# The gated MLP's entry: the scale's scratch moved to another buffer, the late sums queued behind half_x, the last output weights' residues formed by VectorE

## The chip, the cores and the metric

The kernel runs on one core of a Trainium2 chip. The metric is the device time of one execution in microseconds. The core has five engines that each take their instructions in order: TensorE (PE, with its weight load PEld), VectorE (DVE), ScalarE (ACT), GpSimd (POOL) and SyncE (SP, which here issues the DMAs). [...]

## The reference

The kernel computes two layers of a causal decoder over 16 learned meta tokens and 1024 tokens of width 1024. Layer 0 mixes with a short gated convolution and a gated DeltaNet, layer 1 with sliding-window attention. Each layer ends in the part that this change is about, a gated MLP of width 2816 with a causal width-3 convolution on the gate:

```python
def rms_norm(x, w):
    xf = x.astype(jnp.float32)
    y = xf * lax.rsqrt(jnp.mean(xf * xf, -1, keepdims=True) + EPS)
    return (y * w.astype(jnp.float32)).astype(x.dtype)

def conv_ffn(h, w_up, conv_w, w_down):
    gate, val = jnp.split(h @ w_up, 2, -1)
    gate = causal_dwconv(gate, conv_w)
    return (jax.nn.silu(gate) * val) @ w_down
...
for layer in range(DEPTH):
    ...
    h = h + mix.astype(h.dtype)
    ff = conv_ffn(rms_norm(h, ffn_norm_w[layer]), ffn_w_up[layer], ffn_conv_w[layer], ffn_w_down[layer])
    h = h + ff.astype(h.dtype)
```

## The kernel before

Activations lie transposed: eight tiles `h[k]` of 128 channels by 1040 tokens. A float32 product is made of three reduced-precision products: each operand is rounded to a high part (ScalarE) and what is left, the low part, is formed by a subtraction (VectorE or GpSimd); high x high, high x low and low x high are summed in PSUM.

**The MLP (`ffn`).** The tokens are taken as two halves s = 0, 1 of `hf` = 520 (layer 0) or 516 (layer 1) columns. The up projection is done by a seven-product scheme of the Strassen kind: instead of eight block products of inner size 512 there are seven, j = 0 to 6, whose moving operands `X[j][0..3]` are blocks of the normalised input or sums of blocks, and whose weights are blocks of the raw weights `wg`, `wv` or their sums `sa`, `sb`. `parts(j, k, ...)` (L746) makes one operand tile: high part by ScalarE (L750, or L753 with the norm's weight), low part by VectorE (L751 or L754). X0, X1 and X6 come straight from `h`; X2 (`t2`), X3, X4 and X5 need sums by VectorE: L784 and L785 for X2 and X3, L792 for X4, L795 for X5. The 28 operand tiles take five slots of the pool `xb` and slots of `big`, which holds 24 tiles, among them the eight of `h`; slots for the last operands come free only when `h` tiles have been used up.

At the entry also stand the sums of squares for the RMS norm (squares by ScalarE at L740, added up by VectorE in L741, the two halves of a tile `r`), and `scales(s)` (L757) for each half: four matmuls with a matrix of ones into a PSUM tile `C` (L760), then a reciprocal square root by two Newton steps, alternating ScalarE (L763, L764, L766) and VectorE (L767, L768), into `rstd`. Its scratch tiles are `sg`, `th` (which the convolution uses later) and `rs_y`, which has the tag and the one buffer of the snapshot `u2`. `rstd` is first used in L896.

Then a loop over 22 blocks i of 128 hidden channels. Each takes PSUM accumulators from two rings of two, `A` and `C`, and runs its seven products, 24 matmuls each, in this program order: A = X0 (weights w1; snapshot `p1`), C' = X1 (w1; added to `p1` into `r` by L866), A += X2 (w2; snapshot `u2`, a ScalarE copy at L826), C = X3 (w2), A += X4 (w3; snapshot `u3`), then the X0 product of block i+1, A += X5 (w3), C += X6 (w4). A snapshot must be taken before the next product adds to `A`. Weights come by two DMAs per block (L833), are summed (L869, L870, L879, L887), and are split by `wsplit` (high L809, low L810) into a ring of three pairs of tiles. Block 0's and every even block's raw weights share a ring of two buffers with the weight loads of the stage before. The gate then goes through L895, L896, the convolution (L851 to L855) and a multiplication (L898), and a DMA (L899) writes the block to DRAM. The down projection follows in a second part.

**The stage before the second MLP (`swa`).** At its end `outputs(1, yb, QCH[2:])` makes the last 346 tokens of the attention's output projection: four weight loads by `load_w` (L128: DMA L131, high part by ScalarE L134, low part by GpSimd L135, 128x1024 elements), each followed by two groups of 12 matmuls (L147), whose PSUM results VectorE adds into `h` (L1205). Two PSUM buffers are in use there for these groups.

**What sets the order.** The source gives the program order, and a planner that simulates the engines' times chooses the order of instructions within each engine's queue when the program is built, and when buffers are handed on; so instructions of a later line can stand ahead of earlier ones. `with tc.issue_after(ins):` adds one constraint: the instructions of the block that run on `ins`'s own engine come after `ins` in that engine's queue. It adds no semaphore.

Of the kernel before, what the change touches and what calls it, by code (L numbers as in the profile page):

```python
# [2 lines left out]

# [4 lines left out]
F32 = mybir.dt.float32  # L8
# [4 lines left out]
ALU = mybir.AluOpType  # L13
# [5 lines left out]
KT = D // P  # L19
# [8 lines left out]
QCH = [(14, 334)] + CH[1:]  # L28
# [54 lines left out]
def trunk(tc, hT0, w_in, w_ab, w_out, w_q, w_k, w_v, w_o, w_up, w_down, vec, cst, out):  # L83
    nc = tc.nc
    pe, ve, ac, gp, sp = nc.tensor, nc.vector, nc.scalar, nc.gpsimd, nc.sync
    ctx = ExitStack()
    with ctx:
# [38 lines left out]
        def aux(name, tag="b"):  # L126
            return banks["in"].tile([P, 512], F32, tag=tag, name=name, bufs=banks[tag])

        def load_w(src, nk, name):
            raw = wp.tile([P, nk, P], F32, tag="wraw", name=name + "r")  # L130
            sp.dma_start(raw, src)  # L131
            hi = wp.tile([P, nk, P], F32R, tag="whi", name=name + "h")
            lo = wp.tile([P, nk, P], F32R, tag="wlo", name=name + "l")
            ac.copy(hi, raw)  # L134
            gp.tensor_tensor(lo, raw, hi.bitcast(F32), ALU.subtract)  # L135
            return hi, lo

        def gemm(w, xs, c0, n, ks=None, ring=None):
# [567 lines left out]
        def ffn(h, layer, last):  # L706


            hf = 516 if last else 520
# [7 lines left out]
            with tc.tile_pool(name=f"fx{layer}", bufs=5, side="right", reuse_waits="tile") as xb:  # L717
                with tc.tile_pool(name=f"f{layer}", bufs=1, reuse_waits="tile") as fp, \
                        tc.tile_pool(name=f"fu{layer}", bufs=2, space=PSUM, reuse_waits="tile") as pu:

                    def half(tag, bufs, name=None):
                        return fp.tile([P, hf], F32, tag=tag, name=name or tag, bufs=bufs)
# [5 lines left out]
                    def full(tag, bufs=1):  # L728
                        return fp.tile([P, 2 + 2 * hf], F32, tag=tag, name=tag, bufs=bufs)
# [11 lines left out]
                                ve.tensor_tensor(ss[s], ss[s], sq, ALU.add)  # L741

                    X = [[None] * 4 for _ in range(7)]

                    def parts(j, k, src, vcol=None):

                        t = (xb if 4 * j + k < 5 else big).tile([P, T], F32R, tag="big", name=f"X{j}{k}")
                        hi, lo = t[:, 0:hf], t[:, hf:2 * hf]
                        if vcol is None:
                            ac.copy(hi, src)  # L750
                            ve.tensor_tensor(lo, src, hi.bitcast(F32), ALU.subtract)  # L751
                        else:
                            ac.activation(hi, src, AF.Copy, scale=vcol)  # L753
                            ve.scalar_tensor_tensor(lo, src, vcol, hi.bitcast(F32), ALU.mult, ALU.subtract)  # L754
                        X[j][k] = (hi, lo)

                    def scales(s):  # L757
                        ps = wide("C")
                        for b in range(2):
                            pe.matmul(ps[:, b, :q], ones, ss[s][:, b * q:b * q + q], start=True, stop=True)  # L760
                        a, t = (x[:, :hf] for x in (full("sg"), full("th")))
                        y = half("u2", 1, "rs_y")
                        ac.activation(two(a), ps[:, :, :q], AF.Identity, scale=1.0 / D, bias=epsc)  # L763
                        ac.activation(y, a.bitcast(I32), AF.Exp, scale=-0.5 * LN2 / (1 << 23), bias=seed)  # L764
                        for i, (sc, m3) in enumerate(((1.0, -3.00033), (0.25, -0.75))):
                            ac.activation(t, y, AF.Square, scale=sc)  # L766
                            ve.tensor_tensor(t, a, t, ALU.mult)  # L767
                            ve.scalar_tensor_tensor(rstd[:, tk[s]] if i else y, t, m3, y, ALU.add, ALU.mult)  # L768

                    w = [col(V_FN + 8 * layer + k) for k in range(KT)]  # L770

                    B = lambda i, k, s: h[4 * i + k][:, tk[s]]
# [7 lines left out]
                    t2 = [half("t2", 2, "t2") if k < 2 else vt2[:, (k - 2) * hf:(k - 1) * hf] for k in range(4)]  # L780
# [5 lines left out]
                        parts(2, k, t2[k])  # L786
                    for k in range(4):
                        parts(3, k, B(0, k, 0))
                    for s in range(2):
                        scales(s)  # L790
                    for k in range(4):
                        ve.scalar_tensor_tensor(B(0, k, 1), B(1, k, 1), w[4 + k], B(0, k, 1), ALU.mult, ALU.subtract)  # L792
                        parts(4, k, B(0, k, 1))
                    for k in range(4):
                        ve.scalar_tensor_tensor(B(1, k, 0), B(1, k, 0), w[4 + k], t2[k], ALU.mult, ALU.subtract)  # L795
                        parts(5, k, B(1, k, 0))
                        parts(6, k, B(1, k, 1), w[4 + k])

                    nw = [0]

# [6 lines left out]
                    def wsplit(t, at, n, src):  # L807
                        hi, lo = (x[:, at:at + n, :] for x in t)
                        ac.copy(hi, src)  # L809
                        ve.tensor_tensor(lo, src, hi.bitcast(F32), ALU.subtract)  # L810
# [48 lines left out]
                    for i in range(NF):  # L859
                        (wg, wv), w1, A, p1 = nxt  # L860
                        g1, g2, v1, v2 = wg[:, 0:4], wg[:, 4:8], wv[:, 0:4], wv[:, 4:8]
                        Bk = wide("C")
                        product(Bk, w1, 4, 1, True)
                        r = full("r", 2)
                        ve.memset(r[:, 0:2], 0.0)
                        ve.tensor_tensor(two(r[:, 2:2 + hf]), Bk[:, :, :q], two(p1), ALU.add)  # L866

                        sa = fp.tile([P, KT, P], F32, tag="ws", name="sa", bufs=2)
                        ve.tensor_tensor(sa[:, 4:8], v1, v2, ALU.add)  # L869
                        ve.tensor_tensor(sa[:, 0:4], sa[:, 4:8], g1, ALU.subtract)  # L870
                        w2 = wtile()
                        wsplit(w2, 0, KT, sa)
                        product(A, w2, 0, 2, False)
                        u2 = snap("u2", A)
                        C = wide("C")
                        product(C, w2, 4, 3, True)

                        sb = fp.tile([P, KT, P], F32, tag="ws", name="sb", bufs=2)
                        ve.tensor_tensor(sb[:, 0:4], g1, v1, ALU.subtract)  # L879
                        w3 = wtile()  # L880
                        wsplit(w3, 0, 4, sb[:, 0:4])
                        wsplit(w3, 4, 4, v2)
                        product(A, w3, 0, 4, False)
                        u3 = snap("u3", A)
                        v = full("v")
                        ve.tensor_tensor(two(v[:, hf:2 * hf]), two(u3), C[:, :, :q], ALU.subtract)  # L886
                        ve.tensor_tensor(sb[:, 4:8], sa[:, 0:4], g2, ALU.subtract)  # L887
                        if i + 1 < NF:
                            nxt = first(i + 1)
                        product(A, w3, 4, 5, False)  # L890
                        ac.copy(two(v[:, :hf]), A[:, :, :q])
                        w4 = wtile()
                        wsplit(w4, 0, 4, sb[:, 4:8])
                        product(C, w4, 0, 6, False)
                        ve.tensor_tensor(two(r[:, 2 + hf:]), two(u2), C[:, :, :q], ALU.subtract)  # L895
                        ve.tensor_tensor(r[:, 2:], r[:, 2:], rstd[:, o0:], ALU.mult)  # L896
                        sg = conv(i, r)
                        ve.tensor_tensor(sg, sg, v[:, :2 * hf], ALU.mult)  # L898
                        sp.dma_start(yd[i], sg)  # L899
# [37 lines left out]
        def swa(h, sqp):  # L937
# [5 lines left out]
            with tc.tile_pool(name="l1", bufs=1, reuse_waits="tile") as lp:  # L943
# [14 lines left out]
                for i in range(4):  # L958
                    a = lp.tile([P, 192], F32R, name=f"vxh{i}")
# [227 lines left out]
                def parts(G, ys, cs):  # L1187
                    for c0, n in cs:
                        sl = slice(c0, c0 + n)
                        for t in range(4):  # L1190
                            split(ys[t][0][:, sl], ys[t][1][:, sl], qg[G][t][:, sl])

                def outputs(G, ys, cs, pairs=range(4)):
                    for i in pairs:
                        w = load_w(w_o[i, G], 8, "wo")
                        for j in range(2):
                            if G == 0:
                                ho.append(newbig(f"h{2 * i + j}"))

                                gp.memset(ho[-1][:, 8:14], 0.0)  # L1200
                                sp.dma_start(ho[-1][:, 14:], hd[i + 4 * j][:, 14:])
                            t = ho[2 * i + j]
                            for c0, n in cs:
                                ps = gemm([x[:, 4 * j:4 * j + 4] for x in w], ys, c0, n)
                                ve.tensor_tensor(t[:, c0:c0 + n], ps[:, :n], t[:, c0:c0 + n], ALU.add)  # L1205
# [20 lines left out]

                attend(1, hook)
                parts(1, yb, QCH[2:])
                outputs(1, yb, QCH[2:])
            return ho[0::2] + ho[1::2]  # L1230

        with ExitStack() as st:
# [78 lines left out]
```

## Time and profile before

| | us |
|---|---|
| median of 3 runs | 2428.58 (2425.1 to 2428.73) |
| the profiled execution | 2428.64 |
| its span, from the first to the last instruction | 2426.9 |
| TensorE busy / VectorE / ScalarE / GpSimd | 2345.5 / 1656.2 / 981.6 / 483.6 |
| mean granted TensorE clock | 0.989 |
| first MLP: its first product begins | 584.67 |
| second MLP: its first product begins | 1710.03 |

A timeline row has the start, the duration, the engine, the line, the operation with output and inputs, and in brackets how long the engine stood idle before it and what released it. The view of waits adds up such idle time by the waiting line and its releaser: total, times, longest. The view of windows gives, for each stretch, each engine's busy time with the number of instructions, the granted TensorE clock (1.00 is full speed), the DMA engines' busy share and GB/s. In the names, `A<-X,whi` is a product into A from operand X and the weights' high part.

### The profile page before, as it was taken

The numbers are of one execution on the slowest core, as the hardware profiler recorded it, in microseconds if no ns is written. First come the engines' busy times: TensorE is split into PE (matmuls) and PEld (weight loads), VectorE is DVE, ScalarE is ACT, GpSimd is POOL, SyncE is SP. The second block draws the span as 40 slices with busy tenths as digits, with TensorE's granted clock in tenths as the row PEclk, the third lists the DMA queues.
The fourth block names the chain that finished last, engine by engine and source line by source line (L and its number), as shares of the span: only waits on it lengthen the run. The fifth ranks groups of instructions, "written<-read, shape, count | busy, mean of one in ns | idle before, by whom it ended". The sixth has DMA issues, their size and how long they took to land.

```text
span 2426.9 us, 40063 instructions
## 1 busy us (share of the span) xinstructions
PE 2345.5 (97%) x16060; PEld 2214.8 (91%) x16060; DVE 1656.2 (68%) x2836; ACT 981.6 (40%) x1980; POOL 483.6 (20%) x421
## 2 busy tenths in 40 slices
PE   8999999999899999999999999999699999999999
PEld 7989999998899999999999987878699999998887
DVE  8886735667677777785536578778877777778432
ACT  6445213435344444432225456645544444433110
POOL 1113323520000000012225245454000000002221
PEclk9999999999999999999999999999899999999999
DMA  3234434141122222253212100202222222234222
GB/s 136 93 111 133 162 120 142 58 167 71 71 79 79 80 79 79 76 194 114 85 61 106 44 27 19 96 18 82 93 79 79 83 81 80 81 140 159 86 66 100
DMA packets 93481, 224.83 MB, mean 93 GB/s; under 512 B 18672, under 2 KB 30264, under 8 KB 93296
## 3 DMA queue, kind: packets, MB, share of 16 engines
q1 hardware_dynamic: 93296, 222.28, 26.7%
q8 instruction: 126, 2.06, 0.3%
q14 instruction: 59, 0.48, 0.1%
HBM read 166.08 MB, written 56.15 MB: 92 GB/s over the span
## 4 chain that ended last, share of the span: by engine, by line
PE 82%; DVE 12%; ACT 4%; issue 1%; DMA 1%; POOL 0%; SPq 0%; ACTq 0%; DVEq 0%; POOLq 0%
PE mm L147 38%; PE A L820 20%; PE C L820 15%; PE po L1020 1%; DVE qt L251 1%; PE scp L1074 1%; DVE yl L171 1%; ACT sc L1092 1%; DVE X L751 1%; PE qkp L973 0%; ACT xh L182 0%; PE po L1143 0%; DVE Xd L499 0%; DVE wlo L810 0%; DVE fq L497 0%
## 5 line engine op out<-in xcount | busy, mean ns | idle before, releaser
L820 PE MATMUL A<-X,whi 128*128 128x260 f32 (+1 forms) x2816 | 515.3, 284 | 16.4 <-ACT u L826 15.8
L147 PE MATMUL mm<-y,wdh 128*128 128x346 f32 (+2 forms) x1760 | 471.1, 350 | 1.6 <-DVE r L895 1.6
L820 PEld LDWEIGHTS A<-X,whi 128*128 128x128 f32 x2816 | 436.1, 190 | 17.9 <-ACT u L826 17.0
L820 PE MATMUL C<-X,whi 128*128 128x260 f32 (+1 forms) x2112 | 391.5, 284 | 7.7 <-DVE v L886 5.9
L820 PE MATMUL A<-X,wlo 128*128 128x260 f32 (+1 forms) x1408 | 394.2, 283 | 0.0
L135 POOL TENSOR_TENSOR wdl<-wdr,wdh 128x512 fp32r<-128x512 f32 (+1 forms) x80 | 117.8, 1473 | 1301.4 <-ACT wdh L134 1297.0
L147 PEld LDWEIGHTS mm<-y,wdh 128*128 128x128 f32 x1760 | 315.1, 188 | 32.8 <-DVE r L895 2.1
L820 PEld LDWEIGHTS C<-X,whi 128*128 128x128 f32 x2112 | 329.2, 190 | 8.6 <-DVE v L886 6.3
L147 PE MATMUL mm<-y,wdl 128*128 128x346 f32 (+2 forms) x880 | 307.4, 350 | 0.0
L820 PE MATMUL C<-X,wlo 128*128 128x260 f32 (+1 forms) x1056 | 297.2, 283 | 0.0
L820 PEld LDWEIGHTS A<-X,wlo 128*128 128x128 f32 x1408 | 265.6, 190 | 0.0
L931 DVE TENSOR_TENSOR h<-mm,h 128x346 f32<-128x346 f32 (+2 forms) x200 | 115.9, 583 | 208.0 <-PE mm L147 207.5
L820 PEld LDWEIGHTS C<-X,wlo 128*128 128x128 f32 x1056 | 200.0, 190 | 0.0
L147 PEld LDWEIGHTS mm<-y,wdl 128*128 128x128 f32 x880 | 165.5, 188 | 15.4
L810 DVE TENSOR_TENSOR wlo<-sa,whi 128x1024 fp32r<-128x1024 f32 x44 | 53.9, 1225 | 171.4 <-ACT whi L809 171.4
L134 ACT CAST wdh<-wdr 128x512 fp32r<-128x512 f32 (+1 forms) x80 | 53.1, 664 | 265.5 <-PE mm L147 221.1
L809 ACT CAST whi<-sb 128x512 fp32r<-128x512 f32 x88 | 54.6, 621 | 130.2 <-PE C L820 128.4
L147 PE MATMUL mm<-xl,wqkvh 128*128 128x346 f32 (+1 forms) x288 | 96.0, 333 | 1.3 <-DVE xl L183 1.3
L826 ACT COPY u<-A 128x520 f32<-128x520 f32 (+1 forms) x88 | 52.1, 592 | 111.4 <-PE A L820 108.3
L147 PE MATMUL mm<-xh,wqkvh 128*128 128x346 f32 (+1 forms) x288 | 96.2, 337 | 0.7 <-DVE row L269 0.7
L809 ACT CAST whi<-sa 128x1024 fp32r<-128x1024 f32 x44 | 46.1, 1048 | 120.4 <-PE A L820 120.4
L147 PE MATMUL mm<-xh,wqkvl 128*128 128x346 f32 (+1 forms) x288 | 93.3, 326 | 0.0
(401 smaller groups left out, 5259.1 us busy)
## 6 DMA issues: line engine op xcount, KB each, us to landing
wg<-in_w_up SPq DMA_DIRECT2D x44, 512.0 KB, 3.4
wv<-in_w_up SPq DMA_DIRECT2D x44, 512.0 KB, 3.4
wdr<-in_w_down SPq DMA_DIRECT2D x48, 256.0 KB, 2.6
fy<-sg SPq DMA_DIRECT2D x22, 520.0 KB, 2.6
yf<-fy SPq DMA_DIRECT2D x22, 520.0 KB, 4.9
fy<-sg SPq DMA_DIRECT2D x22, 516.0 KB, 2.6
yf<-fy SPq DMA_DIRECT2D x22, 516.0 KB, 4.7
wdr<-in_w_down SPq DMA_DIRECT2D x32, 320.0 KB, 3.0
```

The lines of the kernel that those rows point to most:

```text
L134: ac.copy(hi, raw)
L135: gp.tensor_tensor(lo, raw, hi.bitcast(F32), ALU.subtract)
L147: pe.matmul(ps[:, :n], a[:, j, :], b[:, c0:c0 + n], start=(i == 0), stop=(i == last))
L171: ve.tensor_tensor(dst_l, src, dst_h.bitcast(F32), ALU.subtract)
L251: ve.scalar_tensor_tensor(d, buf[:, pad + c0 - i:pad + c0 - i + n], taps[W - 1 - i], tmp[:, :n], ALU.mult, ALU.add)
L751: ve.tensor_tensor(lo, src, hi.bitcast(F32), ALU.subtract)
L809: ac.copy(hi, src)
L810: ve.tensor_tensor(lo, src, hi.bitcast(F32), ALU.subtract)
L820: pe.matmul(ps[:, b, :q], a[:, at + k, :], x[:, c], start=(start and n == 0), stop=(n == 11), skip_group_check=not start)
L826: ac.copy(two(t), ps[:, :, :q])
L931: ve.tensor_tensor(hn[m][:, s], ps[:, :n], hn[m][:, s], ALU.add)
L1020: pe.matmul(ps, a, b, start=(start and j == 0), stop=(stop and j == 2))
```

## The change

There are three edits.

1. In `scales`, the scratch `y` no longer has a tile of its own with the tag of the snapshot `u2`: it is the second half of the tile `sg`, whose first half is `a`.
2. `half_x` is the VectorE instruction that forms the low part of X3's last tile. The sums for X4 and X5 and the operand tiles X4, X5 and X6, the sums and splits for w3 and w4 of blocks 0 and 1 and those for w2 of block 1 get `issue_after(half_x)`, so what of them runs on VectorE stands behind that instruction in VectorE's queue. The sum `sb[:, 4:8]` (before L887) is written some lines earlier, at the other sum of the same tile, for all blocks.
3. `load_w` takes the engine for the low part, and `outputs` passes it on; the last call, for the last 346 tokens, gives VectorE in place of GpSimd.

```diff
-        def load_w(src, nk, name):
+        def load_w(src, nk, name, eng=gp):
...
-            gp.tensor_tensor(lo, raw, hi.bitcast(F32), ALU.subtract)
+            eng.tensor_tensor(lo, raw, hi.bitcast(F32), ALU.subtract)
...
-                            ve.tensor_tensor(lo, src, hi.bitcast(F32), ALU.subtract)
+                            last_lo[:] = [ve.tensor_tensor(lo, src, hi.bitcast(F32), ALU.subtract).ins]
...
-                        a, t = (x[:, :hf] for x in (full("sg"), full("th")))
-                        y = half("u2", 1, "rs_y")
+                        t = full("th")[:, :hf]
+                        ay = full("sg")
+                        a, y = ay[:, :hf], ay[:, hf:2 * hf]
...
                     for k in range(4):
                         parts(3, k, B(0, k, 0))
+
+                    half_x = last_lo[0]
                     for s in range(2):
                         scales(s)
-                    for k in range(4):
-                        ve.scalar_tensor_tensor(B(0, k, 1), B(1, k, 1), w[4 + k], B(0, k, 1), ALU.mult, ALU.subtract)
-                        parts(4, k, B(0, k, 1))
-                    for k in range(4):
-                        ve.scalar_tensor_tensor(B(1, k, 0), B(1, k, 0), w[4 + k], t2[k], ALU.mult, ALU.subtract)
-                        parts(5, k, B(1, k, 0))
-                        parts(6, k, B(1, k, 1), w[4 + k])
+                    with tc.issue_after(half_x):
+                        for k in range(4):
+                            ve.scalar_tensor_tensor(B(0, k, 1), B(1, k, 1), w[4 + k], B(0, k, 1), ALU.mult, ALU.subtract)
+                            parts(4, k, B(0, k, 1))
+                        for k in range(4):
+                            ve.scalar_tensor_tensor(B(1, k, 0), B(1, k, 0), w[4 + k], t2[k], ALU.mult, ALU.subtract)
+                            parts(5, k, B(1, k, 0))
+                            parts(6, k, B(1, k, 1), w[4 + k])
...
-                        ve.tensor_tensor(sa[:, 4:8], v1, v2, ALU.add)
-                        ve.tensor_tensor(sa[:, 0:4], sa[:, 4:8], g1, ALU.subtract)
                         w2 = wtile()
-                        wsplit(w2, 0, KT, sa)
+                        with tc.issue_after(half_x) if i == 1 else nullcontext():
+                            ve.tensor_tensor(sa[:, 4:8], v1, v2, ALU.add)
+                            ve.tensor_tensor(sa[:, 0:4], sa[:, 4:8], g1, ALU.subtract)
+                            wsplit(w2, 0, KT, sa)
...
-                        ve.tensor_tensor(sb[:, 0:4], g1, v1, ALU.subtract)
                         w3 = wtile()
-                        wsplit(w3, 0, 4, sb[:, 0:4])
-                        wsplit(w3, 4, 4, v2)
+                        with tc.issue_after(half_x) if i < 2 else nullcontext():
+                            ve.tensor_tensor(sb[:, 0:4], g1, v1, ALU.subtract)
+                            ve.tensor_tensor(sb[:, 4:8], sa[:, 0:4], g2, ALU.subtract)
+                            wsplit(w3, 0, 4, sb[:, 0:4])
+                            wsplit(w3, 4, 4, v2)
...
-                        ve.tensor_tensor(sb[:, 4:8], sa[:, 0:4], g2, ALU.subtract)
...
-                        wsplit(w4, 0, 4, sb[:, 4:8])
+                        with tc.issue_after(half_x) if i < 2 else nullcontext():
+                            wsplit(w4, 0, 4, sb[:, 4:8])
...
-                        w = load_w(w_o[i, G], 8, "wo")
+                        w = load_w(w_o[i, G], 8, "wo", eng)
...
-                outputs(1, yb, QCH[2:])
+                outputs(1, yb, QCH[2:], eng=ve)
```

More of the change, by code (lines that the diff above doesn't have):

```diff
@@ L1 @@
 import numpy as np
-from contextlib import ExitStack
+from contextlib import ExitStack, nullcontext
 import concourse.bass as bass
@@ L743, in ffn @@
                     X = [[None] * 4 for _ in range(7)]
+                    last_lo = []
                     def parts(j, k, src, vcol=None):
@@ L1191, in parts, with outputs @@
                             split(ys[t][0][:, sl], ys[t][1][:, sl], qg[G][t][:, sl])
-                def outputs(G, ys, cs, pairs=range(4)):
+                def outputs(G, ys, cs, pairs=range(4), eng=gp):
                     for i in pairs:
-                        w = load_w(w_o[i, G], 8, "wo")
+                        w = load_w(w_o[i, G], 8, "wo", eng)
                         for j in range(2):
```

## The prediction

> **What bounds the kernel now.** I read the page first, then the windows, then TensorE's waits, then the timeline around the longest of them.
>
> ```profile
> PE 2345.5 (97%) x16060; PEld 2214.8 (91%) x16060; DVE 1656.2 (68%) x2836; ACT 981.6 (40%) x1980; POOL 483.6 (20%) x421
> ```
>
> TensorE is the bound; a change gains only where TensorE stands still or runs at a low clock. Inside the MLP's loop it does neither:
>
> ```profile
> 660.00:700.00 40.00, 40.00 (x336) 40.00 (x335) 30.79 (x38) 16.47 (x22) 0.00 (x0) 1.00 0.23 87
> ```
>
> 336 matmuls in 40.00 us are 119 ns each at the full clock, so a product of 24 is 2.9 us and a block of seven 20 us. VectorE (third pair, 30.79) has a quarter of its time free there. So edits that reach every block (the sum written earlier) are costed at nothing: full TensorE is their cover, and without it one sum of 0.68 us would show per block. What is left are the two entries into the MLP. TensorE's waits from 583 to 630 us, then from 1676 to 1760 us (total, times, longest):
>
> ```profile
> PE A L820 <- ACT u L826: 6.5, 2, 5.9
> PE C L760 <- DVE r L741: 2.7, 2, 2.6
> PE C L820 <- DVE r L866: 1.8, 1, 1.8
> PE A L820 <- ACT p L826: 0.6, 1, 0.6
> ```
>
> ```profile
> PE C L760 <- DVE r L741: 7.9, 1, 7.9
> PE A L820 <- ACT u L826: 7.9, 2, 7.2
> PE mm L147 <- DVE h L1205: 6.5, 4, 2.8
> ```
>
> That is 11.6 us and 22.3 us. The longest of the first entry in the timeline:
>
> ```profile
> 598.10 0.41 PE L820 MATMUL A<-X,whi 128*128 128x260 f32 x2
> 613.40 0.70 DVE L768 SCALAR_TENSOR_TENSOR rstd<-th,rs_y 128x520 f32<-128x520 f32 x1
> 614.19 0.59 ACT L826 COPY u<-A 128x520 f32<-128x520 f32 x1 [1.55 <-DVE rstd L768]
> ```
>
> The product X2 ends at 598.5, and its snapshot u2 could be taken then. It is taken at 614.19, right after the last VectorE step of the scales, because that step reads `rs_y`, which lies in u2's buffer. X4 may not add to A before. The stop costs clock too. From the chain that ended last:
>
> ```profile
> 614.84 5.47 PE A L820 x24
> 620.97 3.16 PE A L820 x24
> ...
> 659.59 2.88 PE A L820 x24
> ...
> 1723.29 4.10 PE C L820 x24
> ...
> 1746.15 4.77 PE A L820 x24
> ```
>
> A product that takes 2.9 us warm takes 5.47, 4.10 and 4.77 after the three long stops: 2.6, 1.2 and 1.9 us more.
>
> **Edit 1, the scratch.** It removes no instruction. In the first entry it takes away the stop of 5.9 us and the 2.6 us of slow clock, 8.5 together; in the second 7.2 and 1.9, 9.1. These are bounds, since VectorE may be late next. The new place, the second half of `sg`, adds no wait: `sg` was held for the same scales before, and the convolution, its next user, also needs their result `rstd`.
>
> **What is late next: VectorE.** It runs almost without a pause up to the end of the scales, and is then idle while TensorE works off the delay:
>
> ```profile
> 612.67 0.70 DVE L767 TENSOR_TENSOR th<-sg,th 128x520 f32<-128x520 f32 x1 [0.70 <-ACT th L766]
> ...
> 620.95 0.70 DVE L886 TENSOR_TENSOR v<-u,C 128x520 f32<-128x520 f32 x1 [6.85 <-ACT u L826]
> 625.13 1.23 DVE L810 TENSOR_TENSOR wlo<-sa,whi 128x1024 fp32r<-128x1024 f32 x1 [3.49 <-ACT whi L809]
> ...
> 629.40 1.23 DVE L896 TENSOR_TENSOR r<-r,rstd 128x1040 f32<-128x1040 f32 x1
> ```
>
> So 0.70 + 6.85 + 3.49 = 11.0 us of VectorE are free in the first entry once TensorE doesn't stop. Four VectorE steps of the second half's scales (two turns of L767 and L768, 0.70 each, 2.8 us) may also slide behind the operands, as `rstd` is first read at 629.40.
>
> **Edit 2, the late sums.** It moves work on VectorE's queue. In the first entry much of it was done before 584 us, while TensorE was still full with the mixer and VectorE had time. VectorE's instructions of L792 and L795 from 500 to 584 us, and the sums and splits for w3 and w4 (four from the first to the second row below):
>
> ```profile
> L792 DVE SCALAR_TENSOR_TENSOR h<-h,vt,h x3: 752/2905/2908, 520.4 to 562.1; 128x520 f32<-128x520 f32 x3
> ```
>
> ```profile
> L795 DVE SCALAR_TENSOR_TENSOR h<-h,vt,t x2: 750/752/754, 575.2 to 582.4; 128x520 f32<-128x520 f32 x2
> L795 DVE SCALAR_TENSOR_TENSOR h<-h,vt,v x1: 752/752/752, 583.7 to 583.7; 128x520 f32<-128x520 f32 x1
> ```
>
> ```profile
> 568.29 0.68 DVE L879 TENSOR_TENSOR sb<-wg,wv 128x512 f32<-128x512 f32 x1
> ...
> 571.12 0.68 DVE L887 TENSOR_TENSOR sb<-sa,wg 128x512 f32<-128x512 f32 x1
> ```
>
> Six at 0.75 and four at 0.68 are 7.2 us that now come behind half_x, where VectorE is short. In return X2, X3 and the sums of squares stand earlier. Bounds for the first entry: a gain of 14.2 us if every wait and the slow clock go (11.6 + 2.6), none if the moved work takes everything. I take VectorE's budget, as it is the engine without a pause: 11.0 - 7.2 + 2.8 = **6.6 us**.
>
> The edit issues no DMA itself, but w3's and w4's sums and splits free raw weights for the next load:
>
> ```profile
> 569.60 0.33 SPq L833 DMA_DIRECT2D wg<-in_w_up  x1
> ```
>
> ```profile
> 626.92 1.05 ACT L809 CAST whi<-wg 128x1024 fp32r<-128x1024 f32 x1 [1.33 <-PE C L820]
> ```
>
> ```profile
> wg<-in_w_up SPq DMA_DIRECT2D x44, 512.0 KB, 3.4
> ```
>
> Block 2's load at 569.60 follows the last reader of block 0's `wv`; it will start only after half_x, some 25 to 40 us later. ScalarE first needs it at 626.92, and such a load lands 3.4 us after its issue (the page's last part), so I cost it at nothing; if it comes after 617 us, each us late is one us of TensorE.
>
> **Edit 3, the last four loads.** GpSimd's subtraction holds up VectorE:
>
> ```profile
> 1687.12 2.42 POOL L135 TENSOR_TENSOR wol<-wor,woh 128x1024 fp32r<-128x1024 f32 x1 [8.73 <-ACT woh L134]
> ```
>
> ```profile
> 1674.38 1.37 DVE L171 TENSOR_TENSOR yl<-q,yh 128x346 fp32r<-128x346 f32 x3
> ...
> 1676.10 2.67 DVE L171 TENSOR_TENSOR yl<-q,yh 128x346 fp32r<-128x346 f32 x1
> ...
> 1687.61 2.48 DVE L741 TENSOR_TENSOR r<-r,sq 128x516 f32<-128x516 f32 x1 [0.98 <-ACT sq L740]
> ...
> 1692.79 2.47 DVE L741 TENSOR_TENSOR r<-r,sq 128x516 f32<-128x516 f32 x1 [0.57 <-ACT sq L740]
> ...
> 1698.58 2.86 DVE L792 SCALAR_TENSOR_TENSOR h<-h,vt,h 128x516 f32<-128x516 f32 x1
> ```
>
> The VectorE instruction at 1687.61 ends 0.5 us after GpSimd's at 1687.12 does. Against their usual 0.46, 0.68, 0.68 and 0.75, the four lose 2.2 + 1.8 + 1.8 + 2.1 = 7.9 us. In exchange VectorE does the four subtractions; the row at 625.13 has that size, 1.23 us, so 4.9 us. Net gain 3.0 us of VectorE. Behind each new subtraction in VectorE's queue stand the adds L1205, which hand on the PSUM buffers that TensorE waits for (6.5 us in four waits). Bounds: a loss of 4.9 us, if each subtraction delays such an add in full, to a gain of 6.5 if all four waits go; I take the net 3.0.
>
> **Second entry, the sum.** After its scales VectorE is idle as in the first:
>
> ```profile
> 1743.99 0.70 DVE L767 TENSOR_TENSOR th<-sg,th 128x516 f32<-128x516 f32 x1 [0.70 <-ACT th L766]
> ...
> 1751.56 0.69 DVE L886 TENSOR_TENSOR v<-u,C 128x516 f32<-128x516 f32 x1 [6.14 <-ACT u L826]
> 1755.71 1.23 DVE L810 TENSOR_TENSOR wlo<-sa,whi 128x1024 fp32r<-128x1024 f32 x1 [3.46 <-ACT whi L809]
> ```
>
> That is 10.3 us. Here the moved sums filled no idle time, since VectorE was busy throughout, so nothing is taken off; the wait of 7.9 us for the sums of squares shrinks, as L792, L795 and the splits no longer stand ahead of them. With edit 3's 3.0 and the scales' 2.8 the budget gives 10.3 + 3.0 + 2.8 = **16.1 us**. TensorE's side allows it: 22.3 us of waits and 3.1 of slow clock, 25.4. Bounds: 3.0 (edit 3 alone) to 25.4.
>
> [...]
>
> ```profile
> 1680.00:1690.00 10.00, 9.36 (x48) 9.07 (x48) 7.59 (x11) 4.70 (x7) 2.42 (x1) 0.83 0.10 39
> ```
>
> The clock is at 0.83 here, although no wait before it in this stage is longer than the 2.8 us of the view above. [...]
>
> **Sum.** 6.6 + 16.1 = 22.7 us off the profiled execution's 2428.64: **2405.9 us**. That execution is 1.7 us longer than its span and stands 0.06 us from the median of 2428.58.
>
> **The rivals.**
> - *Every wait goes* (0.13): 14.2 + 25.4 = 39.6, so 2389. For it: u2's wait had no reason but the buffer. Against: VectorE runs without a pause through most of both entries, by its budget above.
> - *X4 replaces the scales* (0.14): the sums for X4, now behind half_x, are what TensorE waits for at the same place. Then edit 3's 3.0 and the slow clock's 2.6 + 1.9 are left, 7.5, so 2421. For it: X4's sums were partly done before 584 us. Against: VectorE's 11.0 and 10.3 us of idle time.
> - *It doesn't do what it says* (0.08): the planner puts u2's copy behind ScalarE's steps of the scales anyway, as ScalarE takes its queue in order. Nothing changes: 2426 to 2429.
> - *Slower* (0.10): a PSUM bank is held. `C` has two buffers; one is kept by the second scales, the other by X1's product until r (L866) has read it, and r's line comes after all late sums. TensorE already waited 1.8 us for it. If the planner puts the whole lump ahead of r, that is 12 instructions at 0.75 and 8 at 0.69 (X4 to X6), 14.5 us, and w3's four, 2.7. X3's first low part:
>
> ```profile
> 592.86 0.69 DVE L751 TENSOR_TENSOR X<-h,X 128x520 fp32r<-128x520 f32 x1
> ```
>
> Four of these end at 595.6; the lump ends at 612.8, r at 613.5, and six products with 2.6 us of slow clock (19.9) end at 633.4. Before, the eighth product ended at 624.1 and the ninth 2.9 later, at 627.0. So 6.4 us are lost there, and with nothing won in the second entry it is 2435. It decides from 10.8 us of VectorE work between half_x and r (595.6 + 10.8 + 0.7 + 19.9 = 627.0). Against it: the planner lets ready instructions pass that stand later in the source, and did so with r.
>
> **How the numbers follow.** The forecast of 2405.9 has 0.55, with 2396 to 2416 of its own from VectorE's budget off by 10 us. Rivals as above. The range of 2388 to 2424 holds the forecast, X4's rival and most of the full gain, and leaves out "nothing" and "slower" (0.18) and a little below. A measurement of this kernel can tell about 0.2%, 4.9 us, from no change. Faster by more: 0.55 + 0.13 + 0.14 = 0.82; within: 0.08; slower: 0.10.
>
> **What would show it.** Edit 1: u2's first copy follows its product within some 2 us, and the wait "A <- ACT u" of 5.9 and 7.2 us is gone. Edit 2: L792 and L795 stand behind X3's low parts; the 7.9 us wait for r L741 is under 4; VectorE has no pause over 3 us between half_x and block 1. Edit 3: no GpSimd work after 1670 until the down projection, no VectorE instruction over 1.3 us there, waits for h L1205 under 4 us in total. Wrong it would be by a new wait of TensorE for X4, for r (L866) or for block 2's weights, or by other waits in the attention stage, whose order the planner may choose anew.

## The result, and the profile after

The changed kernel takes 2406.08 us (median of 4 runs, 2401.72 to 2407.6) against 2426.84 us of the kernel before beside it (4 runs); the ratio is 0.9914, 95% interval 0.9901 to 0.9928. Run again beside the experiments it took 2404.28 us, ratio 0.9907 (0.9893 to 0.9920). The forecast was 2405.9. That the two agree within 0.2 us is partly luck: the forecast took 22.7 us off 2428.64, and what was measured is 20.8 us off 2426.84.

The profiled execution took 2401.72 us, the shortest of the four. Its page, where the line of busy times answers to the one shown of before:

```profile
span 2399.9 us, 40060 instructions
...
PE 2336.4 (97%) x16060; PEld 2205.4 (92%) x16060; DVE 1655.3 (69%) x2840; ACT 982.3 (41%) x1980; POOL 477.0 (20%) x417
```

VectorE has four instructions more and GpSimd four fewer: the four subtractions. TensorE's waits in the changed kernel, first from 583 to 630 us, then from 1660 to 1745 us (total, times, longest):

```profile
PE A L825 <- ACT whi L814: 2.5, 1, 2.5
PE C L825 <- DVE r L871: 1.4, 1, 1.4
PE C L761 <- DVE r L741: 1.0, 1, 1.0
PE A L825 <- ACT u L831: 0.7, 1, 0.7
```

```profile
PE C L761 <- DVE r L741: 9.3, 1, 9.3
PE A L825 <- DVE X L752: 2.0, 2, 1.1
PE A L825 <- DVE wlo L815: 0.6, 1, 0.6
PE C L825 <- DVE X L755: 0.6, 1, 0.6
PE C L825 <- DVE r L871: 0.2, 1, 0.2
```

The lines have moved (L831 is the snapshots' copy, L815 `wsplit`, L871 the addition to `p1`). The first entry's waits fell from 11.6 to 5.6 us. In the second the stops for u2 and for the output adds are gone, 14.4 us, but the one for the last sum of squares grew from 7.9 to 9.3 us. The snapshot u2 in the changed kernel's timeline, with the last rows of X2's product ahead of it:

```profile
591.42 0.41 PE L825 MATMUL A<-X,whi 128*128 128x260 f32 x2
```

```profile
592.22 0.58 ACT L831 COPY u<-A 128x520 f32<-128x520 f32 x1
```

The product ends at 591.8 and the copy starts 0.4 us later; before, it came 15.7 us later. The scales now run on behind it: their last step stands at 619.34.

To see where the time went, the kernel is cut where TensorE passes from one kind of work to another. The groups of matmuls by tile of the changed kernel give the cuts (first and last start in us; the second `wdh` row is of the window from 2100 to 2200 us alone):

```profile
L147 PE MATMUL mm<-yl,wouth x192: 316/321/430, 485.0 to 579.5; 128*128 128x346 f32 x128, 128*128 128x348 f32 x64
```

```profile
L147 PE MATMUL mm<-y,wdh x1760: 315/323/498, 1038.2 to 2395.8; 128*128 128x512 f32 x78, 128*128 128x346 f32 x74, 128*128 128x348 f32 x44
```

```profile
L147 PE MATMUL mm<-yl,woh x192: 310/319/425, 1521.0 to 1685.1; 128*128 128x346 f32 x128, 128*128 128x334 f32 x64
```

```profile
L147 PE MATMUL mm<-y,wdh x140: 388/394/498, 2151.4 to 2199.6; 128*128 128x512 f32 x140
```

The mixer's output ends at 579.5, the first down projection begins at 1038.2, the attention's outputs run from 1521.0 to 1685.1, the second down projection begins at 2151.4. The same cuts for the kernel before and for every experiment, each from its one profile (the rows below "edits 1, 2" are the later experiments, described there):

| kernel | mixer's end | to first down proj. | to first output | outputs | to second down proj. | outputs + last |
|---|---|---|---|---|---|---|
| before | 583.3 | 467.3 | 482.7 | 175.7 | 469.4 | 645.1 |
| changed | 579.5 | 458.7 | 482.8 | 164.1 | 466.3 | 630.4 |
| changed, again | 580.0 | 461.4 | 482.6 | 163.9 | 465.8 | 629.7 |
| edit 1 | 580.0 | 458.3 | 482.6 | 175.6 | 461.8 | 637.4 |
| edit 2 | 581.9 | 471.8 | 482.6 | 169.8 | 473.7 | 643.5 |
| edit 3 | 584.5 | 467.1 | 482.6 | 164.4 | 477.6 | 642.0 |
| edits 2, 3 | 582.6 | 473.7 | 483.2 | 164.6 | 476.0 | 640.6 |
| edits 1, 3 | 582.3 | 455.3 | 482.6 | 164.2 | 465.0 | 629.2 |
| edits 1, 2 | 583.2 | 458.6 | 482.6 | 169.7 | 459.7 | 629.4 |
| changed, low parts doubled | 585.9 | 467.7 | 481.0 | 165.9 | 474.7 | 640.6 |
| changed, scales late | 583.3 | 459.0 | 482.6 | 164.0 | 466.2 | 630.2 |
| edits 1, 3, scales late | 584.4 | 457.1 | 482.5 | 164.4 | 464.4 | 628.8 |
| edits 1, 3, scales and squares late | 578.0 | 458.1 | 481.3 | 164.6 | 465.3 | 629.9 |
| changed, low parts by ScalarE | 585.0 | 460.2 | 483.2 | 164.6 | 463.8 | 628.4 |

The third column is the first entry and its MLP, the last column the second entry with the outputs ahead of it. Of the profiled 27.0 us (2426.9 - 2399.9), 8.6 come from the first entry, 11.6 from the outputs and 3.1 from the second entry; 3.8 are a shorter time up to the mixer's end, which differs between profiles of the same instructions, 578.0 to 585.9 us in the table (last section), and is no gain of the change. Equal code agrees within 0.2 to 3 us in the third column (edit 1 and edits 1, 3: 458.3 and 455.3), within 1 us in the last (changed twice).

### The profile page after: what moved, and what is told of

It is laid out like the page before. It is cut to its first block, busy times and chain, and to the rows that moved or that the text cites. A ratio compares the mean times of both kernels' runs of the same rounds, so it can differ in the third digit from the quotient of the medians.

```text
span 2399.9 us, 40060 instructions
## 1 busy us (share of the span) xinstructions
PE 2336.4 (97%) x16060; PEld 2205.4 (92%) x16060; DVE 1655.3 (69%) x2840; ACT 982.3 (41%) x1980; POOL 477.0 (20%) x417
## 4 chain that ended last, share of the span: by engine, by line
PE 82%; DVE 11%; ACT 3%; DMA 2%; issue 1%; POOL 0%; SPq 0%; ACTq 0%; DVEq 0%; POOLq 0%
PE mm L147 38%; PE A L825 20%; PE C L825 15%; PE po L1028 1%; DVE qt L251 1%; PE scp L1082 1%; ACT sc L1100 1%; DVE yl L171 1%; PE qkp L981 1%; DVE Xd L499 0%; DVE X L752 0%; DVE fq L497 0%; ACT xh L182 0%; PE po L1151 0%; DVE all L1114 0%
## 5 line engine op out<-in xcount | busy, mean ns | idle before, releaser
L147 PEld LDWEIGHTS mm<-y,wdl 128*128 128x128 f32 x880 | 165.5, 188 | 16.1 <-POOL wdl L135 0.7
L815 DVE TENSOR_TENSOR wlo<-sa,whi 128x1024 fp32r<-128x1024 f32 x44 | 53.9, 1225 | 161.4 <-ACT whi L814 161.4
L928 ACT CAST y<-yf 128x346 fp32r<-128x346 f32 (+2 forms) x110 | 54.6, 536 | 91.8 <-DVE yf L927 70.9
```

The lines of the kernel that those rows point to most:

```text
L147: pe.matmul(ps[:, :n], a[:, j, :], b[:, c0:c0 + n], start=(i == 0), stop=(i == last))
L928: ac.copy(yh[:, s], yf[:, s])
```

## The experiments

**Each edit alone, and the change without edit 1.** The edits are those of the diff above, put into the kernel before one at a time.

> Edit 1 alone (the scale's scratch in sg). VectorE's budget: u2's copy no longer waits for the scales, so TensorE's stops of 5.9 us and 7.2 us go with their slow clock (2.6 and 1.9), and VectorE, which keeps its old order, has 11.0 and 10.3 us to spare: about 17 us faster than before, some 2410 us. Rival, the late sums are what gains: X4 takes the place of u2 and edit 1 alone gains under 6 us.

Measured: 2408.17 us, ratio 0.9919 (0.9905 to 0.9932). By the ratio that is 20 us, and nearly all of the change. The table puts 9.0 + 7.7 us of it into the two entries; 3.3 us more of this profile lie ahead of the mixer's end, where edit 1 changes nothing. Its waits in the two entries:

```profile
PE C L760 <- DVE r L741: 2.7, 2, 2.6
PE A L821 <- ACT u L827: 0.4, 1, 0.4
```

```profile
PE C L760 <- DVE r L741: 8.0, 1, 8.0
PE mm L147 <- DVE h L1206: 6.5, 4, 2.8
PE C L821 <- DVE r L867: 0.7, 1, 0.7
```

In the first entry little but the scales' sums is left. The rival, that without the late sums X4 takes u2's place and edit 1 gains under 6 us, is out.

> Edit 2 alone (the late sums behind half_x). VectorE's budget: u2's copy still waits for the last step of the scales, and in the first entry 7.2 us of VectorE work come behind half_x, so nothing is gained: between 2 us faster and 7 us slower than before. Rival, the late sums are what gains: 8 us faster or more.

Measured: 2432.8 us, ratio 1.0023 (1.0015 to 1.0032): by the ratio 5.6 us slower. Its waits:

```profile
PE A L824 <- ACT u L830: 6.6, 2, 5.9
PE C L824 <- DVE r L870: 4.3, 1, 4.3
PE C L824 <- ACT sg L764: 2.6, 1, 2.6
PE C L761 <- DVE r L741: 1.0, 1, 1.0
```

```profile
PE A L824 <- ACT u L830: 10.1, 2, 9.5
PE C L824 <- ACT sg L764: 5.7, 1, 5.7
PE mm L147 <- DVE h L1212: 4.0, 4, 1.8
PE C L761 <- DVE r L741: 2.3, 1, 2.3
PE mm L147 <- POOL wol L135: 0.8, 1, 0.8
```

The stops for u2 are there still (in the second entry longer, 10.1 us for 7.9). The first entry's wait of C for r has grown from 1.8 to 4.3 us, and in both entries a new one has come: C waits for the first step of the second scales (L764). These are the two holders of the two C buffers that the prediction's slower rival named. The stop for the last sum of squares falls from 7.9 to 2.3 us, as the prediction had it for edit 2.

> Edit 3 alone (VectorE forms the low parts of the last four output weights). From the trace of the changed kernel, whose output stage lost all four waits for h L1205: TensorE's outputs end about 11 us sooner, and as VectorE then runs the second entry's work in the old order, most of it stays: 6 to 11 us faster than before. Rival, only VectorE's own time counts (7.9 us of hold-up against 4.9 us of added work): 3 us faster.

Measured: 2421.41 us, ratio 0.9971 (0.9958 to 0.9985), 7 us. In the table TensorE's outputs end 11.3 us sooner, but the second MLP takes 8.2 us longer. Its waits in the second entry tell why:

```profile
PE C L760 <- DVE r L741: 16.0, 1, 16.0
PE A L820 <- ACT u L826: 6.3, 2, 5.6
```

The stop for the sums of squares, 7.9 us before, is 16.0: TensorE comes to it sooner, VectorE does not. Outputs and MLP together gain 3.1 us in this profile, which ran 5 us above the median of its runs; where the rest of the 7 us lies it doesn't show.

> Edits 2 and 3, without edit 1: the scratch stays in u2's buffer. VectorE's budget: u2's copies wait again, in both entries, for the scales, which with the late sums behind half_x end no sooner: TensorE's stops before X4 are back at 5 us or more each, and what is left is edit 3's part, 6 to 11 us faster than before, so some 12 us or more slower than the changed kernel. Rival, the order alone does it: within 5 us of the changed kernel.

Measured: 2426.45 us, ratio 0.9992 (0.9984 to 1.0001): no gain is shown without edit 1. The expected 6 to 11 us were missed: by the ratios edit 2's loss of 5.6 us and edit 3's gain of 7.0 nearly cancel.

**The change without edit 2, without edit 3, and with work added.** These ran beside the changed kernel, on the same chip.

> The changed kernel itself, beside the next ones on the same chip: 0.986 to 0.994 of before, about 2407 us.

Measured: 2404.28 us, ratio 0.9907 (0.9893 to 0.9920).

> Edits 1 and 3, without edit 2. Alone, edit 1 gained 20 us and edit 3 gained 7, edit 2 lost 5. If the parts add up, this is 27 us faster than before, some 2401 us, and 5 us faster than the changed kernel. Rival, VectorE's budget as predicted: edit 3's freed time and edit 1 draw on the same idle time of VectorE, and edit 2 is what turns it into earlier operands: 0 to 5 us slower than the changed kernel.

Measured: 2401.45 us, ratio 0.9897 (0.9883 to 0.9910). The interval overlaps that of the changed kernel, so which of the two is faster stays open; that edit 2 makes the change faster is not shown by it. Its waits in the second entry are one line:

```profile
PE C L760 <- DVE r L741: 14.6, 1, 14.6
```

With the late sums ahead, VectorE reaches the last sum of squares later, but after it TensorE waits for nothing more. With them behind (the changed kernel) the stop is 9.3 us, and 3.4 us of small waits follow, most of them for late operands; in its second profile they are 8.7 and 1.8 us. The last column of the table has 629.2 and 630.4: the same time in two forms.

> Edits 1 and 2, without edit 3. If the parts add up: 15 us faster than before, some 2413 us. If edit 2 only costs while u2 holds TensorE up, and helps once that is gone: 20 us faster or more, 2408 us or less.

Measured: 2408.93 us, ratio 0.9926 (0.9912 to 0.9940). Against edit 1 alone (0.9919) no difference can be told. In the last column of the table edits 1, 2 stand at 629.4 and edits 1, 3 at 629.2, where edit 1 alone stands at 637.4: in these single profiles either edit gives 8 us there, and both together no more. The medians of the runs don't show this for edit 2.

> The changed kernel with the low parts of X4 and X5 formed twice (the second time the same values): 8 more VectorE instructions of 0.61 us behind half_x in each entry, 4.9 us. VectorE's budget: VectorE is the bound of both entries, so each added us is one us later: 8 to 11 us slower than the changed kernel. Rival, TensorE's order and fixed waits are the bound (r L741 in the second entry, the snapshots): under 4 us slower.

```diff
                             last_lo[:] = [ve.tensor_tensor(lo, src, hi.bitcast(F32), ALU.subtract).ins]
+                            if j in (4, 5):
+                                ve.tensor_tensor(lo, src, hi.bitcast(F32), ALU.subtract)
```

Measured: 2420.11 us, ratio 0.9975 (0.9966 to 0.9985): 16 us slower than the changed kernel beside it, more than the 9.8 us of work that were added. The waits of the first entry:

```profile
PE C L827 <- DVE v L896: 4.0, 1, 4.0
PE A L827 <- ACT whi L816: 2.6, 1, 2.6
PE C L827 <- DVE r L873: 1.4, 1, 1.4
PE C L763 <- DVE r L741: 1.0, 1, 1.0
PE A L827 <- ACT u L833: 0.7, 1, 0.7
```

Four lines are those of the changed kernel, the first is new: 4.0 us. What else this entry lost is, as far as the windows show, the clock. Behind this stop it is low again:

```profile
606.00:626.00 20.00, 15.27 (x105) 14.67 (x105) 18.76 (x31) 9.39 (x15) 0.00 (x0) 0.83 0.07 27
```

The column before the last two is the granted clock: 0.83 over 20 us, and 3.4 us of clock are missing. The first entry with its MLP took 467.7 us, 6 to 9 more than in the changed kernel's two profiles; the second with its outputs took 640.6, 10 to 11 more. This profile is the slowest of its nine runs, 6 us above their median.

**The stop for the sums of squares.** The prediction had it shrink, and it grew. In the queue of TensorE the second scales' matmuls (L761) stand ahead of X1's product, whose operands are long ready.

> The changed kernel with the second half's scales called after block 0's X1 product. In the changed kernel TensorE stops 9 us in the second entry for the last sum of squares, though X1 and its weights are ready: X1's product stands behind the scales' matmuls in the queue. If that order holds TensorE up, X1's product runs in the stop: 3 to 5 us faster than the changed kernel, some 2401 us. If VectorE's work is the bound, TensorE meets the later operands sooner and waits for them instead: within 2 us of it.

```diff
-                    for s in range(2):
-                        scales(s)
+                    scales(0)
...
                         product(Bk, w1, 4, 1, True)
+                        if i == 0:
+                            scales(1)
```

Measured: 2407.81 us, ratio 0.9926 (0.9914 to 0.9938), against 0.9907 of the changed kernel: not faster. Its two longest waits in the second entry:

```profile
PE C L761 <- DVE r L741: 6.1, 1, 6.1
PE A L824 <- DVE wlo L814: 3.2, 1, 3.2
```

The stop shrank by 3 us, and a new one of 3.2 us took its place: X4's product waits for the low part of w3, whose sum is one of the late ones.

> Edits 1 and 3 with the second half's scales after block 0's X1 product. Here the stop is 14.6 us and VectorE has all later operands ready when it ends. If the order holds TensorE up: 3 to 4 us faster than without this step (X1's product, 2.9 us, and its slow clock, 1.7), 2398 us. X2's product still can't start, as the snapshot p1 has the buffer of the last square. If VectorE is the bound: no change, 2401.

Measured: 2403.4 us, ratio 0.9904 (0.9891 to 0.9917); edits 1 and 3 alone had 0.9897. No change. The stop of 14.6 us is gone, and in the second entry stand instead:

```profile
PE A L820 <- ACT whi L809: 5.4, 1, 5.4
PE A L820 <- DVE wlo L810: 4.9, 1, 4.9
PE C L820 <- DVE h L1207: 0.8, 1, 0.8
```

The planner has moved block 1's first product ahead, and the two long waits are that product's, for the high and the low part of its weights.

> As the one before, and the second half's squares in a buffer of the convolution's input tile in place of p1's. Then p1 can be taken and X2's product can start once X2 is there. If the order and the snapshot's buffer hold TensorE up: 3 to 6 us faster than the one before, 2393 to 2396. If VectorE is the bound: no change against it.

```diff
+                    sq1 = full("r", 2)[:, :hf]
...
-                                sq = half("p1", 1, "sq") if s else half("u3", 1, "sq")
+                                sq = sq1 if s else half("u3", 1, "sq")
```

Measured: 2403.78 us, ratio 0.9906 (0.9891 to 0.9920). Again no change, and again other waits (p1 3.7 us, low parts of weights 3.6). In the table the three late orders have 628.8 to 630.2 in the last column, like the kernels that they start from. So the place of the stop isn't what it costs: TensorE waits for what VectorE and ScalarE have still to do behind the last output, at whichever product it stands.

**Work taken away behind half_x.**

> The changed kernel with the low tiles of X4 and X5 written by a ScalarE copy in place of VectorE's subtraction: the residue of these two operands is not computed, 8 VectorE instructions of 0.61 us (4.9 us) go from each entry, and ScalarE gets as many. VectorE as the bound of both entries: 7 to 12 us faster than the changed kernel, 2392 to 2399, the mirror image of the doubled subtractions. If those 15 us were not VectorE's time but a disturbed order: within 4 us of the changed kernel.

```diff
+                            if j in (4, 5):
+                                ac.copy(lo, src)
+                            else:
-                            last_lo[:] = [ve.tensor_tensor(lo, src, hi.bitcast(F32), ALU.subtract).ins]
+                                last_lo[:] = [ve.tensor_tensor(lo, src, hi.bitcast(F32), ALU.subtract).ins]
```

Measured: 2407.1 us, ratio 0.9914 (0.9900 to 0.9928), no faster than the changed kernel. The expectation of 7 to 12 us was wrong. Its longest wait in the first entry and in the second:

```profile
PE C L828 <- DVE r L874: 4.3, 1, 4.3
```

```profile
PE C L764 <- DVE r L741: 9.4, 1, 9.4
```

In the second entry the stop of 9.4 us stands before half_x, and work behind half_x has no part in it; after it the changed kernel waits for 3.4 us only. The table has 1 to 2 us less there than for the changed kernel. In the first entry TensorE waits 4.3 us for r, which hands on a C buffer. In the changed kernel it stands still equally long between X2 and X3 (from 591.8 to 596.1 us); one matmul of X4 in between splits that into the waits of 2.5 and 1.4 us. In both kernels r begins 7.8 us after VectorE has gone on from half_x, and the subtractions that were taken away stand behind r. So less work there gains next to nothing because it stands behind each entry's longest stop, while more of it, the doubled subtractions, made a new stop of 4.0 us and cost clock (0.83 over 20 us). What less work ahead of r would gain isn't shown, nor what it would be without the eight copies that ScalarE got in return.

## Why the prediction was right

**Edit 1.** Right: in the first entry u2 is taken 0.4 us after its product, and in both entries the long stop for it is gone, with the slow clock after it (before, 0.50 from 614 to 620 us and from 1746 to 1748). The changed kernel has slow clock elsewhere, behind the stops that are left: 0.51 from 596 to 598 us, 0.50 from 1698 to 1702. The prediction gave edit 1 bounds of 8.5 and 9.1 us; alone it gained 9.0 in the first entry (467.3 to 458.3; equal code differs by up to 3) and 7.7 in the second (645.1 to 637.4). It is nearly the whole of the change: 0.9919 alone, 0.9992 without it.

**VectorE's budget in the first entry.** 6.6 us were forecast; the two profiles show 8.6 and 5.9. The term of edit 2, 7.2 us against VectorE, had the right sign: alone, edit 2 lengthens the first entry by 4.5 us (467.3 to 471.8), and together with edit 1 and with or without edit 3 the changed order takes 458.6 to 461.4 where the old one took 458.3 and 455.3. That is 0 to 6 us, so the size isn't settled. In return the wait for the sums of squares in the first entry fell from 2.7 to 1.0 us.

**The second entry.** 16.1 us were forecast; outputs and MLP together gained 14.7 and 15.4. The total held, but three of its terms did not, and that they made up for one another is luck: without edit 3 the same sum gives 13.1 us, and edits 1, 2 gained 15.7 in their profile; edits 1, 3 gained 15.9. Edit 3 was sized as VectorE's net time, 3.0 us; it took all four waits away, 6.5 us, and the slow clock among them (from 1680 to 1690 us 0.83 before, 1.00 in the changed kernel), and TensorE's outputs end 11.6 us sooner. Most of that was not kept: with edit 3 alone 8.2 us went back into a longer stop for the sums of squares, because VectorE's work up to the last sum is what TensorE then waits for. So the step "the wait of 7.9 us for the sums of squares shrinks" failed, and so did its check ("under 4"). Edit 2 does shorten it, from 7.9 us to 2.3 (edit 2 alone, and edits 1, 2) and from 14.6 (edits 1, 3) to 9.3 (all three), but edit 3 had brought TensorE to it sooner than I counted. And the step that gave edit 2 a use failed: the shorter stop is paid back in waits for the late operands, and the time is the same without edit 2.

**VectorE as the bound.** True in one direction only. Added work of 4.9 us per entry cost 16 us in all, through stops and the clock (in the first entry a new stop of 4.0 us, and 0.83 over 20 us); the same work taken away gained nothing that the runs can tell, as it stood behind the longest stops. What bounds the second entry is, as far as the runs show, the work from the last output to X2, X3 and the scales, which edits 2 and 3 shift but don't shorten by more than 8 us, and the three late orders (scales late, squares late) not at all. Up to the stop's end it is VectorE's: in the changed kernel's timeline VectorE has no pause from 1684.11 us until the last sum of squares begins at 1697.90. That less of this work would end the stop sooner is argued and not shown: no run took work away before half_x.

**The rivals.** X4 in u2's place: out in its size, but not nil. X4's product waits 2.5 us in the first entry, for the high part of w3, whose sum (592.96 us) now stands behind half_x, and 0.95 us in the second for its own operand; u2's longest stops there were 5.9 and 7.2. "It doesn't do what it says": out. "Every wait goes": out, 9.3 us stayed. The slower rival, a held C buffer: not in its size, as 7.8 us of VectorE's work lie between half_x and r (587.6 to 595.4), under its threshold of 10.8; the rows, with the two waits that follow, are

```profile
585.15 2.53 DVE L752 TENSOR_TENSOR X<-h,X 128x520 fp32r<-128x520 f32 x4
587.59 2.77 DVE L797 SCALAR_TENSOR_TENSOR h<-h,vt,h 128x520 f32<-128x520 f32 x4
...
595.39 0.69 DVE L871 TENSOR_TENSOR r<-C,p 128x520 f32<-128x520 f32 x1
```

```profile
594.35 0.39 PE L825 MATMUL A<-X,whi 128*128 128x260 f32 x1 [2.53 <-ACT whi L814]
596.14 0.80 PE L825 MATMUL C<-X,whi 128*128 128x260 f32 x2 [1.40 <-DVE r L871]
```

X3's product waits 1.4 us for r. Both waits come from edit 2's order, and behind them the granted clock is 0.51 from 596 to 598 us; edits 1, 3 have neither wait and the shortest first entry, 455.3 us. The held buffer is real all the same: with edit 2 alone C waits 4.3 and 2.6 us for its two holders in the first entry, where it waited 1.8 before, and the kernel is 0.23% slower.

**What else was to show.** Block 2's weights, whose load moved from 569.60 to 594.32 us, were not waited for, as forecast. VectorE has no pause over 0.9 us behind half_x in either entry (3 were allowed). GpSimd has no work between 1654.8 us and the second MLP, and no VectorE instruction there is longer than 1.3 us, as forecast. TensorE runs through the outputs without a stop and at the full clock:

```profile
1657.00:1686.00 29.00, 29.00 (x179) 28.27 (x179) 26.09 (x47) 17.99 (x28) 0.00 (x0) 1.00 0.59 209
```

No version among the runs clearly beats the changed kernel. Edits 1 and 3 without edit 2 have the lowest median, 2401.45 us, and are the simpler code.

## What to carry to other kernels

A scratch tile that shares its one buffer with a snapshot puts the snapshot behind everything that uses the scratch; look for a wait whose releaser has nothing to do with the data. When several edits act on one stage, add them up against the stage's slowest chain and not each by its own wait: here, in single profiles, two edits were worth the same 8 us, and the wait that one of them removed came back at the next product. Putting an engine's late work behind its early work gains only if nothing waits for the late work in turn; here the waits moved from the sums of squares to X4's weights and to r. Try the order without such an edit before keeping it.

## What the runs showed of the hardware that I had not expected

The same instructions up to the mixer's end took from 578.0 us (edits 1 and 3 with late scales and squares) to 585.9 us (doubled subtractions) in profiles of kernels that differ only behind them or in VectorE's late sums. Most of it arises between 100 and 200 us, as the windows of those two kernels show:

```profile
100.00:200.00 100.00, 97.58 (x614) 93.45 (x613) 82.54 (x141) 43.34 (x89) 22.37 (x13) 1.00 0.38 123
```

```profile
100.00:200.00 100.00, 95.51 (x585) 91.40 (x583) 80.37 (x136) 42.06 (x86) 21.13 (x13) 0.97 0.37 121
```

In the first the granted clock stays at 1.00, in the second it falls to 0.97, and 29 fewer matmuls are done, which at the 0.16 us from one to the next in such a stage (100.00 us for 614) is 4.6 us. By an estimate from these rows some 3 us of that are the lower clock (0.03 of 100 us) and 2.1 us are longer pauses of TensorE (busy 97.58 against 95.51). That is near to what edit 2 costs or edit 3 gains alone, so single profiles were compared by stages and not by their spans. What lowers the clock in one of these profiles and not in the other, the runs don't show.

The clock also made a stop cost more than its length: in the second entry of the changed kernel the 9.3 us stop is followed by slow matmuls.

```profile
1694.00:1698.00 4.00, 0.00 (x0) 0.00 (x0) 4.00 (x8) 2.48 (x4) 0.00 (x0) 0.50 0.00 0
1698.00:1702.00 4.00, 3.35 (x11) 2.98 (x12) 4.00 (x7) 3.95 (x8) 0.00 (x0) 0.50 0.00 0
1702.00:1706.00 4.00, 4.00 (x36) 4.00 (x35) 4.00 (x8) 3.67 (x6) 0.00 (x0) 1.00 0.00 0
```

At a clock of 0.50, 11 matmuls are done in 3.35 us; at 1.00, 36 in 4.00. Four of the 11 are the scales': they took 2.09 us (at 1698.65), where the same four of the first entry took 1.14 (at 584.68, the clock at 1.00 from 584 to 588 us).
